# Latent attention: second group's keys scaled ahead of the first group's last two heads, rotated key parts stored with zeros for the neighbouring head

## The chip, the cores and the metric

The kernel runs on one core of one Trainium2 chip. The metric is the device time of one execution in microseconds (us). The kernel before takes 2076.73 us (median of 3 runs, 2075.65 to 2081.17).

## The reference

Two transformer blocks over one sequence of 256 tokens, width 1024, in float32: a short convolution, a dense feed-forward layer, latent attention, a mixture of 8 experts, then feed-forward layers around block attention and a state-space mixer. The change touches latent attention alone:

```python
def mla_mixer(h, cos, sin, w_down, q_a_norm, kv_a_norm, w_uq, w_ukv, q_norm, k_norm, w_o):
    ...
    q = (c_q @ w_uq).reshape(bsz, seq, N_HEADS, QK_HEAD_DIM)          # 8 heads, 128 + 64
    kv = (c_kv @ w_ukv).reshape(bsz, seq, N_HEADS, QK_NOPE_DIM + V_HEAD_DIM)
    k = jnp.concatenate([k_nope, k_rope_h], axis=-1)                  # 64 rotated values, shared
    q = rmsnorm(q, q_norm)
    k = rmsnorm(k, k_norm)
    ...
        scores = jnp.einsum('bqhd,bkhd->bhqk', q[:, s0:end], k[:, :end])
        p = jax.nn.softmax(jnp.where(mask, scores, neg), axis=-1)
        outs.append(jnp.einsum('bhqk,bkhd->bqhd', p, v[:, :end]))
    return o @ w_o
```

A head's score is a product over 128 plain values plus a product over 64 rotated values.

## The kernel before

Projections run as three float32r products of split operands (a high and a low part: ScalarE makes the high part of a weight with a CAST, VectorE the low part with a subtraction, both 128x1024). Scores, transposes and the products with the values run in float32. Every instruction goes through one recording layer, so all of them carry line L149 and are told apart by their tiles.

**Who sets the order.** The order on each engine is fixed when the program is built, by a planner. `Clock` keeps a planned time for each engine; for each recorded instruction it adds a cost from `Clock.cost` (lines 89 to 107) and notes when its tiles are written. For GpSimd (POOL) that cost is the line

```python
        return 0.16 if op == "tensor_scalar" else 0.3 + n * 0.165
```

with n the elements of one partition. `Pipe` (line 276) holds items, each a few stages with names that have to be done first. While the projections are written out, `Pipe.tick` places a stage among them once the planned time says that its inputs are ready (`self.ready(item) <= t["tensor"] + SLACK`). Where a name is needed and nothing is ready, `Pipe.force` places the open stage whose inputs are planned to be ready first. At most 6 items may be started at once. On the chip each engine then runs its instructions strictly in that order; only semaphores make it wait.

**Latent attention** (`mla`, line 1214) takes the heads in two groups g = 0, 1 of four, and the tokens in two tiles t = 0, 1 of 128. For each group: `uq` and `ukv` multiply by the weights, ScalarE evacuates the banks, VectorE sums squares; `norm` then adds two items for each tile. `q_scales` takes roots on POOL and rotates the queries on VectorE; `q_turn` transposes them on TensorE (four 128x128 transposes of the plain parts, two of the rotated parts, two heads in each) and ScalarE copies them to `qn` and `r`. `scales` takes the keys' roots on POOL, `keys` multiplies the keys by them on VectorE, and `turn` transposes the keys to `kn` and `r`.

Each head (`head`, line 1136) has four stages: `scores` (products on TensorE, maximum and bias on VectorE, exponential on ScalarE), `normalise` (VectorE), `transpose` (TensorE, then a copy by VectorE) and `values` (TensorE, then a CAST by ScalarE and a subtraction by VectorE). A score takes for both tiles a product over 128 partitions (`qn`, `kn`), a product over 64 partitions of `r` (partitions 0 to 63 for even heads, 64 to 127 for odd ones), and two bf16 products that add the mask. Line 1439 asks for head 0, and `out_proj` (line 659) multiplies head after head by `w_o` (tile `dn<-s`, 128x512, 12 products for each of heads 0 to 3), waiting for each head by name. The pool of `acc` banks and the pool of `dn` banks have 4 banks each; during `out_proj` the heads use `acc`.

Of the kernel before, what the change touches and what calls it, by code (L numbers as in the profile page):

```python
# [539 lines left out]
class K:  # L540
# [673 lines left out]
    def mla(self, cur, ph):  # L1214
        nc, ws, pipe = self.nc, self.ws, self.pipe
        ws.limit(NSLOT - 7)
        self.lent.clear()
        tsl = lambda t: slice(t * 128, (t + 1) * 128)
# [4 lines left out]
        kr = self.sm([128, 2, 64], "kr")  # L1223
# [47 lines left out]
        for j, n in ((0, 384), (1, 320)):  # L1271
            held = []
            for t in range(2):
                if j == 0 and t:
                    cur.need(1)
                ps = self.lend(("cp", t, j))[:, :n]
                for q in range(4):
                    if t == 0:
                        held.append(ws.get())
                    p = held[q]  # L1280
# [5 lines left out]
        ws.use = 2  # L1286


        q, kv = {}, {}
        rqs = self.sm([128, 2, 8], "rq")  # L1290
        rks = self.sm([128, 2, 8], "rk")
        big = {}

        def tiles(g):
            for t in range(2):
                s = self.slot([128, 1792])
                q[t, g] = s[:, 0:768].rearrange("p (a b) -> p a b", a=4)
                kv[t, g] = s[:, 768:1792].rearrange("p (a b) -> p a b", a=4)

        def uq(g, j):  # L1300
            h = 4 * g + 2 * j
            ps = [self.lend(("uq", t, h))[:, :384] for t in range(2)]
            c = 0
            while c < 3:
                p = ws.get()
                for t in range(2):
                    if g == 0 and j == 0:
                        pipe.need(("lat", t, 0))
                    for i in range(p.n):
                        self.mm3(ps[t], (ch[0][:, c + i, tsl(t)], cl[0][:, c + i, tsl(t)]),  # L1310
                                 (p.h[:, i, :], p.l[:, i, :]), c + i == 0, c + i == 2)
                    pipe.tick()
                c += p.n

            def evac(t):
                qq = q[t, g][:, 2 * j:2 * j + 2, :]

                def copy():
                    nc.scalar.activation(qq, ps[t].rearrange("p (a b) -> p a b", a=2), AF.Copy, scale=ra[:, t, 0:1])

                def squares():
                    for i in range(2):
                        junk = self.t2()
                        nc.vector.scalar_tensor_tensor(junk[:, :192], qq[:, i, :], 1.0, qq[:, i, :], op0=ALU.mult,
                                                       op1=ALU.mult, accum_out=rqs[:, t, h + i:h + i + 1])

                pipe.add([copy], ("uq", t, h), after=(("sq", t, 0),))
                pipe.add([Stage(squares, inputs=lambda: [qq])], ("uqs", t, h), after=(("uq", t, h),))

            for t in range(2):  # L1330
                evac(t)
# [29 lines left out]
        def norm(t, g):  # L1361
            hs = slice(4 * g, 4 * g + 4)
            st = {}

            def q_scales():
                b = rqs[:, t, hs]
                self.rsqrt(b, b, 1.0 / 192)
                nc.gpsimd.tensor_scalar(b, b, 192 ** -0.5, None, op0=ALU.mult)
                st["qr"] = self.t2((128, 4, 64))
                self.rope(st["qr"], q[t, g][:, :, 128:192], tab[:, t, 0], 4, 32)  # L1370

            def scales():
                a = rks[:, t, hs]
                nc.gpsimd.tensor_scalar(a, a, krs[:, t:t + 1], None, op0=ALU.add)
                self.rsqrt(a, a, 1.0 / 192)

            def keys():
                rb = rks[:, t, hs, None]
                kn = kv[t, g][:, :, 0:128]
                nc.vector.tensor_tensor(kn, kn, rb.to_broadcast([128, 4, 128]), op=ALU.mult)  # L1380
                st["kr"] = krh = self.t2((128, 4, 64))
                nc.vector.tensor_tensor(krh, kr[:, t, None, :].to_broadcast([128, 4, 64]),
                                        rb.to_broadcast([128, 4, 64]), op=ALU.mult)

            def rot(n, m):
                src = [st[n][:, 2 * i:2 * i + 2, :] for i in range(2)]
                ps = self.side()
                for i in range(2):
                    nc.tensor.transpose(ps[:, i * 128:(i + 1) * 128], src[i], self.ident)
                nc.scalar.copy(big["r"][:, m, 2 * g:2 * g + 2, tsl(t)],  # L1390
                               ps[:, 0:256].rearrange("p (a b) -> p a b", a=2))

            def q_turn():
                if not big:
                    big["qn"], big["kn"] = self.slot([128, 8, 256]), self.slot([128, 8, 256])
                    big["r"] = self.slot([128, 2, 4, 256])
                self.trans_heads(big["qn"][:, hs, tsl(t)], [q[t, g][:, i, 0:128] for i in range(4)],
                                 lambda o, s: nc.scalar.activation(o, s, AF.Copy, scale=self.gqk))
                rot("qr", 0)

            def turn():
                self.trans_heads(big["kn"][:, hs, tsl(t)], [kv[t, g][:, i, 0:128] for i in range(4)],
                                 lambda o, s: nc.scalar.copy(o, s))
                rot("kr", 1)

            h = 4 * g
            pipe.add([q_scales, q_turn], ("nq", t, g), after=(("uqs", t, h), ("uqs", t, h + 2)))
            pipe.add([scales, keys, turn], ("nk", t, g), after=(("ukvs", t, h), ("ukvs", t, h + 2), ("nq", t, g)))

        out = {}  # L1410

        def score(h, t):
            b = 64 * (h % 2)
            ke = 128 * (t + 1)
            r = big["r"]
            return [(big["qn"][:, h, tsl(t)], big["kn"][:, h, :ke]),
                    (r[b:b + 64, 0, h // 2, tsl(t)], r[b:b + 64, 1, h // 2, :ke])]

        def heads(g):
            if not out:  # L1420
                out["h"], out["l"] = self.slot([128, 8, 256], F32R), self.slot([128, 8, 256], F32R)
            for h in range(4 * g, 4 * g + 4):
                pipe.add(self.head(h, score, [rqs[:, 0, :], rqs[:, 1, :]],
                                   lambda h, kt: kv[kt, h // 4][:, h % 4, 128:256], out["h"], out["l"],
                                   lambda h=h: [big["qn"][:, h, :], big["kn"][:, h, :], big["r"][:, :, h // 2, :]]),
                         (ph, h), after=[(n, t, g) for n in ("nq", "nk") for t in range(2)])

        for g in range(2):
            ws.limit((12, 9)[g], 2)
            tiles(g)  # L1430
            uq(g, 0)
            uq(g, 1)
            ukv(g)
            for t in range(2):
                norm(t, g)
            heads(g)
# [755 lines left out]
```

## Time and profile before

| what | before |
|---|---|
| median of 3 runs | 2076.73 us (2075.65 to 2081.17) |
| profiled execution, its own time | 2080.76 us |
| its span | 2078.9 us |
| TensorE (PE) busy | 2057.5 us (99%) |
| VectorE (DVE) busy | 1480.5 us (71%) |
| ScalarE (ACT) busy | 1164.8 us (56%) |
| GpSimd (POOL) busy | 70.7 us (3%) |
| mean granted TensorE clock | 0.997 of full speed |

PE is busy nearly all the time, so the span is PE's work plus PE's waits. A piece of work off PE counts only where PE waits for it. Latent attention's projections and heads lie between about 292 and 383 us of the span.

### The profile page before, as it was taken

Reading aid. Unit: us, or ns where it says so; the run is one execution under the profiler, and the core shown is the slowest. Engines: PE = TensorE matmul, PEld = TensorE weight load, DVE = VectorE, ACT = ScalarE, POOL = GpSimd, SP = SyncE. Lnnn points to the kernel's source line nnn. Section 1 sums busy time; section 2 is a strip of 40 time slices with the busy share of each in tenths; the row PEclk is TensorE's granted clock in tenths of the full one; section 3 lists DMA queues with packets and bytes.
Section 4 is the critical chain, followed back from the end, with each engine's and each line's share of the span. In section 5 each row is a group of like instructions: output and inputs, shape, how many; then the busy total and the mean of one; then the engine's idle time right before and its main releaser. Section 6 shows DMA issues by size and latency. Waiting matters only on the chain.

```text
span 2078.9 us, 27430 instructions
## 1 busy us (share of the span) xinstructions
PE 2057.5 (99%) x10790; PEld 1752.3 (84%) x10790; DVE 1480.5 (71%) x2051; ACT 1164.8 (56%) x1580; POOL 70.7 (3%) x134
## 2 busy tenths in 40 slices
PE   9999999999999999999999999999999999999999
PEld 9988897888888888887888888888888799988888
DVE  7764567799999999898644787455545588884544
ACT  5444446677777777776544555444444446663442
POOL 0000013000000000000000110000000000010000
PEclk9999999999999999999999999999999999999999
DMA  9565422699999999997856337554655144367530
GB/s 365 189 229 184 147 94 75 241 359 324 372 372 321 374 346 350 375 334 258 306 171 196 126 103 273 188 186 134 231 184 174 50 142 128 117 226 260 183 101 21
DMA packets 203867, 457.81 MB, mean 220 GB/s; under 512 B 10675, under 2 KB 25298, under 8 KB 203730
## 3 DMA queue, kind: packets, MB, share of 16 engines
q1 hardware_dynamic: 203698, 455.97, 62.9%
q8 instruction: 86, 1.41, 0.3%
q14 instruction: 51, 0.42, 0.1%
q10 hardware_dynamic: 32, 0.01, 0.0%
HBM read 454.90 MB, written 1.05 MB: 219 GB/s over the span
## 4 chain that ended last, share of the span: by engine, by line
PE 52%; DVE 0%; ACT 0%; issue 0%; POOL 0%; ACTq 0%
PE acc L149 35%; PE dn L149 17%; ACT s L149 0%; DVE t L149 0%; DVE s L149 0%; POOL gr L149 0%; ACT t L149 0%; DVE x L149 0%; DVE gr L149 0%; DVE pf L149 0%; ACTq L149 0%
## 5 line engine op out<-in xcount | busy, mean ns | idle before, releaser
L149 PE MATMUL acc<-s 128*128 128x512 f32 (+3 forms) x6640 | 1318.7, 356 | 8.5 <-ACT s L149 6.3
L149 PEld LDWEIGHTS acc<-s 128*128 128x128 f32 (+1 forms) x6640 | 1097.1, 189 | 181.5 <-ACT s L149 8.8
L149 DVE TENSOR_TENSOR s<-s 128x1024 fp32r<-128x1024 f32 (+3 forms) x914 | 1041.1, 1184 | 186.2 <-ACT s L149 181.7
L149 ACT CAST s<-s 128x1024 fp32r<-128x1024 f32 (+1 forms) x881 | 867.2, 1040 | 298.1 <-DVE s L149 124.9
L149 PE MATMUL dn<-s 128*128 128x512 f32 (+3 forms) x2888 | 646.6, 381 | 0.2 <-DVE s L149 0.2
L149 PEld LDWEIGHTS dn<-s 128*128 128x128 f32 (+2 forms) x2888 | 507.1, 185 | 102.5 <-issue 3.5
L149 DVE TENSOR_TENSOR s<-acc,s 128x512 fp32r<-128x512 f32 (+1 forms) x102 | 62.2, 635 | 221.3 <-ACT s L149 221.3
L149 ACT ACTIVATE t<-acc,rs 128x512 f32<-128x512 f32 (+1 forms) x68 | 44.3, 657 | 180.9 <-PE acc L149 175.8
L149 DVE SCALAR_TENSOR_TENSOR t<-acc,rs,t 128x512 f32<-128x512 f32 (+1 forms) x60 | 42.2, 705 | 62.9 <-PE acc L149 62.9
L149 ACT CAST s<-acc 128x512 fp32r<-128x512 f32 (+1 forms) x102 | 52.2, 545 | 59.6 <-PE acc L149 59.6
L149 ACT ACTIVATE t<-acc,rsl 128x512 f32<-128x512 f32 x32 | 22.0, 689 | 78.6 <-PE acc L149 78.6
L149 POOL TENSOR_TENSOR rs<-ss 128x1 f32<-128x1 f32 x20 | 5.6, 280 | 1547.1 <-ACT t L149 970.7
L149 PE MATMUL acc<-cst,t 128*128 128x128 f32 x376 | 52.0, 272 | 0.0
L149 PEld LDWEIGHTS acc<-cst,t 128*128 128x128 f32 x376 | 44.7, 140 | 7.4
L149 ACT CAST s<-t 128x512 fp32r<-128x512 f32 (+2 forms) x44 | 26.3, 604 | 41.4 <-DVE t L149 41.2
L149 DVE SCALAR_TENSOR_TENSOR t<-acc,gall,t 128x255 f32<-128x255 f32 (+3 forms) x112 | 42.8, 450 | 6.5 <-ACT t L149 6.4
L149 ACT COPY s<-dn 128x256 f32<-128x256 f32 (+2 forms) x45 | 17.5, 420 | 47.8 <-PE dn L149 47.8
L149 ACT ACTIVATE t<-x 128x512 bf16<-128x512 f32 x40 | 25.1, 628 | 28.3 <-DVE x L149 24.6
L149 DVE TENSOR_TENSOR s<-t,s 128x512 fp32r<-128x512 f32 (+2 forms) x44 | 29.0, 669 | 14.6 <-ACT s L149 14.1
L149 DVE TENSOR_TENSOR t<-acc,gall 128x512 f32<-128x512 f32 x32 | 21.6, 688 | 16.2 <-PE acc L149 16.2
L149 ACT ACTIVATE s<-dn,gall 128x256 fp32r<-128x256 f32 x32 | 13.1, 476 | 26.9 <-PE dn L149 26.9
L149 ACT ACTIVATE t<-t 128x512 f32<-128x512 f32 (+1 forms) x17 | 10.5, 621 | 29.0 <-DVE t L149 29.0
(194 smaller groups left out, 746.9 us busy)
## 6 DMA issues: line engine op xcount, KB each, us to landing
s<-in_moe_w_gate_dram SPq DMA_DIRECT2D x64, 1024.0 KB, 6.1
s<-in_moe_w_up_dram SPq DMA_DIRECT2D x64, 1024.0 KB, 6.2
s<-in_moe_w_down_dram SPq DMA_DIRECT2D x64, 1024.0 KB, 5.3
s<-in_ffn_w_gate_dram SPq DMA_DIRECT2D x55, 1024.0 KB, 5.2
s<-in_ffn_w_up_dram SPq DMA_DIRECT2D x55, 1024.0 KB, 5.2
s<-in_ffn_w_down_dram SPq DMA_DIRECT2D x55, 1024.0 KB, 5.0
s<-in_ssm_w_in_dram SPq DMA_DIRECT2D x24, 1024.0 KB, 5.1
s<-in_attn_w_qkv_dram SPq DMA_DIRECT2D x12, 1024.0 KB, 5.2
```

The costliest lines, as they stand in the source:

```text
L149: return real(out, *args, **kw)
```

## The change

Four edits, all in `mla`:

- Each head's rotated keys get a 128-partition block of their own in `r` (now 8 blocks instead of 4 shared ones): 64 partitions hold the key, the other 64 hold zeros. Two POOL memsets of 64 partitions by 4x256 elements write the zeros once; `turn` writes the keys with two copies of 64 partitions in place of one of 128.
- The rotated queries of two heads stay together in one 128-partition tile, `qr`, which lies in the tile of q and kv (now 2048 elements wide instead of 1792).
- A score's second product so runs over 128 partitions, as the first does; the zeros take out the neighbouring head.
- The keys' item is split: `scales` and `keys` no longer wait for the queries' `q_turn`, and heads 2 and 3 now also wait for `keys` of group 1.

```diff
-                s = self.slot([128, 1792])
+                s = self.slot([128, 2048])
...
+                qr[t, g] = s[:, 1792:2048].rearrange("p (a b) -> p a b", a=2)
...
             def q_turn():
                 if not big:
                     big["qn"], big["kn"] = self.slot([128, 8, 256]), self.slot([128, 8, 256])
-                    big["r"] = self.slot([128, 2, 4, 256])
+
+                    big["r"] = self.slot([128, 8, 256])
+                    pairs = big["r"].rearrange("p (a b) c -> p a b c", b=2)
+                    for i in range(2):
+                        nc.gpsimd.memset(pairs[64 - 64 * i:128 - 64 * i, :, i, :], 0.0)
...
-                rot("qr", 0)
+                nc.scalar.copy(qr[t, g], rot("qr"))
...
-                rot("kr", 1)
+                ps = rot("kr")
+                pairs = big["r"][:, hs, tsl(t)].rearrange("p (a b) c -> p a b c", b=2)
+                for i in range(2):
+                    r = slice(64 * i, 64 * i + 64)
+                    nc.scalar.copy(pairs[r, :, i, :], ps[r])
...
-            pipe.add([scales, keys, turn], ("nk", t, g), after=(("ukvs", t, h), ("ukvs", t, h + 2), ("nq", t, g)))
+            pipe.add([scales, keys], ("keys", t, g), after=(("ukvs", t, h), ("ukvs", t, h + 2)))
+            pipe.add([turn], ("nk", t, g), after=(("keys", t, g), ("nq", t, g)))
...
-                    (r[b:b + 64, 0, h // 2, tsl(t)], r[b:b + 64, 1, h // 2, :ke])]
+                    (qr[t, h // 4][:, h % 4 // 2, :], big["r"][:, h, :ke])]
...
-                         (ph, h), after=[(n, t, g) for n in ("nq", "nk") for t in range(2)])
+                         (ph, h), after=[(n, t, g) for n in ("nq", "nk") for t in range(2)] +
+                         [("keys", t, 1) for t in range(2) if h in (2, 3)])
```

Outside latent attention no engine's order changes, and the order of loads on SP's queue is the same throughout. Three places show what moves.

**PE at head 0's scores.** Before, from the last mask product of head 0 (`dn_3129`) on:

```order
L149 MATMUL dn_3129<-mbf_1321,idbf_1323 128x128
L149 MATMUL dn_3146<-s_2946,s_2945 128x128
L149 MATMUL dn_3146<-s_2946,s_2945 128x256
L149 MATMUL dn_3146<-s_2947 128x128
L149 MATMUL dn_3146<-s_2947 128x256
```

With the change, from the last mask product of head 0 (`dn_3119`) on; `t2_3129` is head 0's exponential, `t2_3143` its transposed copy, `s_2872` its output and `s_3012` the first part of `w_o`:

```order
L149 MATMUL dn_3119<-mbf_1321,idbf_1323 128x128
L149 MATMUL dn_3139<-cst_73,t2_3129 128x128 x3
L149 MATMUL dn_3145<-t2_3143,s_2720 128x256
L149 MATMUL dn_3145<-t2_3143,s_2721 128x128
L149 MATMUL dn_3150<-s_3012,s_2872 128x512 x2
L149 MATMUL dn_3150<-s_3012,s_2873 128x512
```

Before, heads 1, 2 and 3 follow head 0's scores; now head 0's own transposes, values and output products do.

**DVE after the last sum of squares of group 0's keys.** Before (`s<-s,rk` and `t<-kr,rk` are one tile's `keys`, `s<-s 128x1024` the low part of a weight, `SCALAR_TENSOR_TENSOR ..,rq` a head's sum of squares):

```order
L149 TENSOR_TENSOR s<-s,rk 128x4x128
L149 TENSOR_TENSOR t_2962<-kr,rk 128x256
L149 SCALAR_TENSOR_TENSOR t_2964,rq<-s 128x192
L149 SCALAR_TENSOR_TENSOR t_2966,rq<-s 128x192
L149 SCALAR_TENSOR_TENSOR t_2968,rq<-s 128x192
L149 SCALAR_TENSOR_TENSOR t_2970,rq<-s 128x192
L149 TENSOR_TENSOR s<-s 128x1024 x3
L149 TENSOR_TENSOR s<-s,rk 128x4x128
L149 TENSOR_TENSOR t_3034<-kr,rk 128x256
```

With the change:

```order
L149 TENSOR_TENSOR s<-s,rk 128x4x128
L149 TENSOR_TENSOR t_2967<-kr,rk 128x256
L149 TENSOR_TENSOR s<-s,rk 128x4x128
L149 TENSOR_TENSOR t_2991<-kr,rk 128x256
L149 SCALAR_TENSOR_TENSOR t_3004,rq<-s 128x192
L149 SCALAR_TENSOR_TENSOR t_3006,rq<-s 128x192
L149 SCALAR_TENSOR_TENSOR t_3008,rq<-s 128x192
L149 SCALAR_TENSOR_TENSOR t_3010,rq<-s 128x192
L149 TENSOR_TENSOR s<-s 128x1024 x3
L149 SCALAR_TENSOR_TENSOR t_3054,rq<-s 128x192
L149 SCALAR_TENSOR_TENSOR t_3056,rq<-s 128x192
L149 TENSOR_TENSOR s<-s 128x1024 x2
```

Both tiles' `keys` of group 0 now stand together, and five low parts of weights stand ahead of head 0's maximum instead of three.

**DVE behind the last head's scores.** Before (`su` and the tensor-scalar rows normalise a head, `COPY t<-acc` copies a head's transposes, `s<-acc,s` is the low part of a head's output):

```order
L149 RECIPROCAL su<-su 128x2
L149 TENSOR_SCALAR t_3333<-t_3333,su 128x128
L149 TENSOR_SCALAR t_3333<-t_3333,su 128x256
L149 TENSOR_TENSOR s<-s 128x1024
L149 TENSOR_TENSOR s<-acc,s 128x256
L149 COPY t_3410<-acc 128x384
L149 COPY t_3416<-acc 128x384
L149 COPY t_3422<-acc 128x384
L149 TENSOR_TENSOR s<-s 128x1024
L149 TENSOR_TENSOR s<-acc,s 128x256 x3
```

With the change:

```order
L149 RECIPROCAL su<-su 128x2
L149 TENSOR_SCALAR t_3362<-t_3362,su 128x128
L149 TENSOR_SCALAR t_3362<-t_3362,su 128x256
L149 COPY t_3391<-acc 128x384
L149 COPY t_3397<-acc 128x384
L149 COPY t_3403<-acc 128x384
L149 COPY t_3409<-acc 128x384
L149 COPY t_3415<-acc 128x384
L149 COPY t_3421<-acc 128x384
L149 TENSOR_TENSOR s<-acc,s 128x256 x6
```

Six heads (2 to 7) now go through each stage together: on PE six score groups stand in a row, then six groups of transposes, then values of head 2, output products, and the values of heads 3 to 7.

## Rows read from the trace of the kernel before

**Rows 1.** Page, part 1: busy time, share of the span, instructions.
```profile
PE 2057.5 (99%) x10790; PEld 1752.3 (84%) x10790; DVE 1480.5 (71%) x2051; ACT 1164.8 (56%) x1580; POOL 70.7 (3%) x134
```

**Rows 2.** Timeline, PE: start us, us, engine, operation, count, [idle before <-releaser].
```profile
326.72 0.60 PE L149 MATMUL dn<-cst,s 128*128 128x128 f32 x4
...
338.38 0.66 PE L149 MATMUL dn<-cst,s 128*128 128x128 f32 x4 [1.03 <-ACT s L149]
...
341.07 1.72 PE L149 MATMUL dn<-s 128*128 128x128 f32 x8
342.72 0.28 PE L149 MATMUL dn<-mbf,idbf 128*128 128x128 bf16 x2
...
348.17 0.63 PE L149 MATMUL dn<-cst,s 128*128 128x128 f32 x4 [1.60 <-DVE s L149]
...
372.96 2.12 PE L149 MATMUL acc<-t,s 128*128 128x256 f32 x12
374.84 7.76 PE L149 MATMUL dn<-s 128*128 128x512 f32 x33
...
1648.31 0.73 PE L149 MATMUL acc<-s 128*128 128x512 f32 x2 [1.36 <-ACT s L149]
```

**Rows 3.** Windows: stretch, us, busy us of PE, PEld, DVE, ACT, POOL, then PEclk.
```profile
349.00:349.50 0.50, 0.41 (x3) 0.43 (x3) 0.46 (x3) 0.50 (x2) 0.00 (x0) 0.64 0.00 0
...
352.50:353.00 0.50, 0.50 (x4) 0.49 (x4) 0.00 (x0) 0.00 (x0) 0.00 (x0) 0.95 0.00 0
...
1650.00:1652.00 2.00, 2.00 (x9) 1.62 (x7) 0.00 (x0) 0.00 (x0) 0.36 (x1) 0.50 0.00 0
```

**Rows 4.** Groups by line and form, POOL, whole span: busy us, mean ns.
```profile
masks.py:197 POOL MEMSET cst<- 128x128 f32 x1 | 0.2, 204 | 0.3 <-POOLq L2179 0.3
```

**Rows 5.** Timeline, DVE, latent attention.
```profile
327.93 0.68 DVE L149 TENSOR_TENSOR s<-s,rk 128x512 f32<-128x512 f32 x1
...
328.87 0.35 DVE L149 SCALAR_TENSOR_TENSOR t<-s 128x192 f32<-128x192 f32 x1
...
329.98 3.49 DVE L149 TENSOR_TENSOR s<-s 128x1024 fp32r<-128x1024 f32 x3
...
335.44 0.82 DVE L149 TENSOR_TENSOR t<-s 128x256 f32<-128x256 f32 x3
336.30 0.43 DVE L149 TENSOR_TENSOR t<-t,t 128x256 f32<-128x256 f32 x1
...
341.27 0.62 DVE L149 TENSOR_REDUCE mx<-dn 128x1 f32<-128x128 f32 x2 [1.63 <-PE dn L149]
...
351.38 0.55 DVE L149 TENSOR_SCALAR t<-t,su 128x128 f32<-128x128 f32 x2
351.84 0.55 DVE L149 COPY t<-dn 128x384 f32<-128x384 f32 x1
...
374.87 0.43 DVE L149 TENSOR_TENSOR s<-acc,s 128x256 fp32r<-128x256 f32 x1 [0.23 <-ACT s L149]
```

**Rows 6.** Timeline, POOL: the last step of the keys' roots, group 0, tile 1.
```profile
329.08 1.03 POOL L149 TENSOR_TENSOR rk<-rk,mhalf 128x4 f32<-128x4 f32 x1
```

**Rows 7.** Timeline, ACT, latent attention.
```profile
328.19 2.97 ACT L149 CAST s<-s 128x1024 fp32r<-128x1024 f32 x3
331.04 1.07 ACT L149 ACTIVATE s<-acc,mra 128x384 f32<-128x384 f32 x2
...
342.07 1.28 ACT L149 ACT_TABLE_LOAD   x1 [1.77 <-DVE nb L149]
...
344.26 0.20 ACT L149 ACTIVATION_READ_ACCUMULATOR t<-dn,nb,rq 128x1 f32 x1
...
374.46 0.37 ACT L149 CAST s<-acc 128x256 fp32r<-128x256 f32 x1 [0.28 <-PE acc L149]
```

**Rows 8.** Timeline, PEld (weight loads of PE), within head 0's scores.
```profile
340.09 0.52 PEld L149 LDWEIGHTS dn<-s 64*128 64x128 f32 x4 [0.33 <-issue]
340.94 0.11 PEld L149 LDWEIGHTS <-idbf 128*128 128x128 bf16 x2 [0.33 <-issue]
```

More of the change, by code (lines that the diff above doesn't have):

```diff
@@ L1286, in mla @@
         ws.use = 2
-        q, kv = {}, {}
+        q, kv, qr = {}, {}, {}
         rqs = self.sm([128, 2, 8], "rq")
@@ L1383, in keys, with rot @@
                                         rb.to_broadcast([128, 4, 64]), op=ALU.mult)
-            def rot(n, m):
-                src = [st[n][:, 2 * i:2 * i + 2, :] for i in range(2)]
+            def rot(n):
                 ps = self.side()
                 for i in range(2):
-                    nc.tensor.transpose(ps[:, i * 128:(i + 1) * 128], src[i], self.ident)
-                nc.scalar.copy(big["r"][:, m, 2 * g:2 * g + 2, tsl(t)],
-                               ps[:, 0:256].rearrange("p (a b) -> p a b", a=2))
+                    nc.tensor.transpose(ps[:, i * 128:(i + 1) * 128], st[n][:, 2 * i:2 * i + 2, :], self.ident)
+                return ps[:, 0:256].rearrange("p (a b) -> p a b", a=2)
             def q_turn():
@@ L1403, in turn @@
                                  lambda o, s: nc.scalar.copy(o, s))
-                rot("kr", 1)
+                ps = rot("kr")
[3 more added lines that the diff above has]
+                    nc.scalar.copy(pairs[r, :, i, :], ps[r])
             h = 4 * g
             pipe.add([q_scales, q_turn], ("nq", t, g), after=(("uqs", t, h), ("uqs", t, h + 2)))
-            pipe.add([scales, keys, turn], ("nk", t, g), after=(("ukvs", t, h), ("ukvs", t, h + 2), ("nq", t, g)))
+            pipe.add([scales, keys], ("keys", t, g), after=(("ukvs", t, h), ("ukvs", t, h + 2)))
+            pipe.add([turn], ("nk", t, g), after=(("keys", t, g), ("nq", t, g)))
         out = {}
         def score(h, t):
-            b = 64 * (h % 2)
             ke = 128 * (t + 1)
-            r = big["r"]
             return [(big["qn"][:, h, tsl(t)], big["kn"][:, h, :ke]),
-                    (r[b:b + 64, 0, h // 2, tsl(t)], r[b:b + 64, 1, h // 2, :ke])]
+                    (qr[t, h // 4][:, h % 4 // 2, :], big["r"][:, h, :ke])]
         def heads(g):
@@ L1424, in heads @@
                                    lambda h, kt: kv[kt, h // 4][:, h % 4, 128:256], out["h"], out["l"],
-                                   lambda h=h: [big["qn"][:, h, :], big["kn"][:, h, :], big["r"][:, :, h // 2, :]]),
-                         (ph, h), after=[(n, t, g) for n in ("nq", "nk") for t in range(2)])
+                                   lambda h=h: [big["qn"][:, h, :], big["kn"][:, h, :], big["r"][:, h, :], qr[0, h // 4],
+                                            qr[1, h // 4]]),
+                         (ph, h), after=[(n, t, g) for n in ("nq", "nk") for t in range(2)] +
+                         [("keys", t, 1) for t in range(2) if h in (2, 3)])
         for g in range(2):
```

## The prediction

> **What bounds the kernel now.** The page's busy times come first: PE is busy for 2057.5 us, 99% of the span [rows 1]. So I look at PE's work, PE's waits and PE's clock in the stage that the change touches, and at other engines only where PE waits for them. PE's timeline there [rows 2] shows two waits of over 1 us: 1.03 us before group 1's first keys are evacuated (338.38) and 1.60 us before group 1's scaled keys (348.17). The reader is also to see in it a head's scores (341.07 to about 342.85, 1.78 us), three heads' products with the values (372.96 to 374.84, 0.63 us a head) and 33 output products in 7.76 us (0.235 us each). The windows [rows 3] show what followed the 1.60 us wait: the granted clock falls to its lower level (1.2 of 2.4 GHz) for seven half-microseconds, of which the first and the last stand there with 0.64 and 0.95. With 0.50 in the five or so between, about 1.7 us are lost. The same follows the 1.36 us wait at 1648.31: 0.50 in the window from 1650 [rows 2, 3].
>
> **Why the order comes out as it does.** The edit's words promise keys that are ready earlier. But the order is the planner's, and the planner charges a memset by its rule for POOL, 0.3 + 0.165 for each element: 1024 elements make 169 of its microseconds, the two 338. A memset of 128 elements takes 0.204 us on the chip [rows 4]. I estimate 0.2 to 1.6 us each for 1024 elements (as long as that one, or eight times it) and take 1 us; nothing waits for them, since head 0's scores, the first to read the zeros, come some 8 us later. In the planner's books, though, POOL is late by hundreds of microseconds, and so is all that needs group 1's roots. With nothing planned to be ready, stages are placed by force, one head after the other. The order shows it: behind head 0's scores PE gets no other head, but head 0's own transposes.
>
> **The change part by part.** PE's matmuls are the same in number. So the sum is: PE's waits after less waits before, the clock, and what the scores gain. I follow PE from 326.72, up to where both orders agree.
>
> *Turns of group 0.* The four turns now stand together, ahead of the projections that filled the gaps. Six transposes take about 0.7 us (four show 0.60, and ends overlap) [rows 2]. The first queries' turn ends at 327.4; the keys of tile 0 are scaled at 327.93 + 0.68 = 328.6 [rows 5]: 1.1 us wait. Tile 1's keys need POOL's roots, which end at 329.08 + 1.03 = 330.1 [rows 6], and 0.68 us on DVE: 330.8, where PE is ready at 330.0: 0.8 us. Together 1.9 us; PE goes on at 331.5. The four extra 64-partition copies on ACT cost at most the 0.3 us or so of a 128-partition copy each, and are in the next step.
>
> *Banks.* ACT is through with the turns at about 332.3, then makes three casts (2.97 us) before it evacuates group 1's second query bank (1.07 us for two) [rows 7]: 335.8. PE, after six products of 384 columns and twelve of 512, wants that bank at 335.3: 0.5 us. Twelve more products and head 0's scores end at 340.2.
>
> *Head 0, the largest term.* DVE now has to do, from 331.1 on and ahead of head 0's maximum: eight sums of squares of queries (328.87 to 329.98 is four, 1.1 us), five low parts (three take 3.49 us, so 5.8), two rotations (0.82 and 0.43 overlapping, 1.2 us each) and eight shorter sums of squares (at most 0.28 us each, I take 2.0 in all) [rows 5]. That is 12.4 us, and 1 us more until ACT's first cast is there: 344.5. From the start of a maximum to the end of the exponential it is 341.27 to 344.46, 3.2 us with the table load of 1.28 us [rows 5, 7], then 0.6 us until the first half is normalised: 348.3. PE has waited 8.1 us. The copy of the transposes (0.55 us) and the cast of the output (0.37 us) [rows 5, 7] are waited for in turn, with semaphores 1.0 us. Term: 9.1 us. Before, three more heads' scores covered this chain. If DVE were on time, 4.9 us would be left.
>
> *Head 1.* Its chain without the table load takes 1.9 + 0.6 us; two queries' turns of group 1 (1.4 us) lie beside it. Left are 1.1 us, then copy and cast, 1.0 us, and 0.2 us for the second tile's keys, which DVE scales only then: 2.3 us.
>
> *Heads 2 to 7.* Six score groups stand in a row and PE is busy. Call their end T. DVE then takes the last maximum and bias (0.9 us) and normalises six heads at 0.65 us each (0.46 us between the rows at 351.38 and 351.84, and a reciprocal) [rows 5]. PE waits 1.5 us for the first, 0.3 us for each of the next three. The fifth head's transposes need a bank that DVE's copy of the first frees, and DVE makes that copy only after the sixth normalisation, at T + 5.4: 1.5 us. Then 0.2 us for banks, 0.45 us for a cast, and 0.25 us for the low part of head 2's output, which stands behind all six copies (T + 8.15). Term: 4.8 us.
>
> *Clock.* The fall behind the 1.60 us wait goes with it. The waits at head 0 and behind T are longer than the two that a fall followed [rows 2, 3]; I take two falls, 1.7 us each: 3.4 in place of 1.7. Bounds: none to four, 0 to 6.8 us.
>
> *Scores.* The 64-partition group begins after a gap of 0.33 us in the weight loads, and the mask's loads come after another [rows 8]. Without the change of shape a head could take two times the 0.63 us that the products with the values take for the same 128 + 256 columns, and 0.13 us for the mask: 1.39 for 1.78 us [rows 2]. Bounds 0 and 0.39 us a head; I take 0.39, since that row is of the same size and operand type, for the seven heads on PE's path (head 0's is hidden behind DVE): 2.7 us.
>
> A rule speaks against the padding. The Trainium skill, TensorEngine Tiling (Array Packing), Overview, gives up to twice the speed to products over 64 rows or fewer. By that rule the zeros would give away half of the 0.85 us that a 64-row group takes, 3.4 us over 8 heads, where I count a gain of 2.7. The trace doesn't bear it out: the group takes 0.85 us (340.09 to 340.94), more than 0.63 [rows 2, 8].
>
> **The sum.** Waits after: 1.9 + 0.5 + 9.1 + 2.3 + 4.8 = 18.6 us. Waits before: 1.03 + 1.60 = 2.6. So +16.0; the clock +1.7; the scores -2.7: **+15.0 us**. The profiled execution took 2080.76 us, 4.0 more than the median of 2076.73, and would come to 2095.8. Set on the median: **2091.7 us**. Later stages keep their order, and PE is their bound, so nothing is won back.
>
> **The rivals.**
> - *Faster.* The short scores (8 x 0.39 = 3.1 us) and the end of the two waits and of the clock's fall (1.03 + 1.60 + 1.7) decide: 2076.7 - 7.4 = 2069.3 us. It needs DVE to be through with its list when head 0's scores end, and a softmax chain below 1 us. The rows make it 3.8 us, and nothing stands beside it on PE. Chance 0.04.
> - *No difference to be measured* (0.3%, 6.2 us, is about what a measurement can tell). DVE is on time (head 0: 4.9), head 1 costs 1, the tail 2, no clock fall: 10.3 - 2.6 - 1.7 - 2.7 = +3.3, 2080.0 us. Against it stands DVE's list. Chance 0.09.
> - *The clock stays low.* With wait after wait, the lower level lasts from head 0 into head 1, and 7 us of work there take 14: 2099 us. For it: both the 1.36 and the 1.60 us wait were followed by a fall, and the new ones are longer. Chance 0.11.
> - *Narrow products are fast.* The rule on 64 rows holds: 15.0 + 2.7 + 3.4 = +21.1, 2097.8 us. Against it stands the row. Chance 0.03.
> - *The memsets are as slow as planned.* Head 0's scores wait: some 2410 us. Against it stand the 0.204 us. Chance 0.01.
>
> **How the numbers follow.** The forecast keeps 0.72. Its own bounds are the head 0 term without DVE's lag and no fall (+7, 2084) and four falls with no gain in the scores (+21, 2098). The range of 2083 to 2102 takes in the low clock and the narrow products, and leaves out 0.14. Faster by over 0.3%: 0.04; within: 0.09; slower: 0.87.
>
> **What would show it.** Right: a PE wait of some 8 us for DVE (`t`) just behind head 0's scores, with no other head between; DVE busy meanwhile with low parts and squares; a row of waits behind the last scores; 64-row loads gone and heads 1.4 us apart; memsets of about 1 us. Wrong: DVE's maximum right behind head 0's scores, waits below 10 us in all between 326 and 395, or a span that grows outside that stretch.

## The result, and the profile after

The changed kernel took 2098.32 us (median, 2096.24 to 2099.43), the kernel before beside it 2078.53 us: a ratio of 1.0094, 95% interval [1.0082, 1.0106], or 19.8 us more. The forecast was 15.0 us more. The profiled execution took 2097.98 us with a span of 2096.2, 17.3 us over the span before.

The page's busy times say little. PE has 5 us more, ACT's extra instructions are the half-width copies, POOL has the two memsets:

```profile
PE 2062.4 (98%) x10790; PEld 1757.8 (84%) x10790; DVE 1480.9 (71%) x2051; ACT 1166.9 (56%) x1584; POOL 72.7 (3%) x136
```

PE's timeline of the stage, where [rows 2] stood before (start us, us, engine, operation, count, idle before and what ended it):

```profile
325.86 0.60 PE L149 MATMUL dn<-cst,s 128*128 128x128 f32 x4
...
327.81 0.66 PE L149 MATMUL dn<-cst,s 128*128 128x128 f32 x4 [1.13 <-DVE s L149]
...
330.44 0.63 PE L149 MATMUL dn<-cst,s 128*128 128x128 f32 x4 [1.10 <-DVE s L149]
...
335.95 3.03 PE L149 MATMUL acc<-s 128*128 128x512 f32 x12 [0.84 <-ACT s L149]
338.82 1.47 PE L149 MATMUL dn<-s 128*128 128x128 f32 x8
340.13 0.27 PE L149 MATMUL dn<-mbf,idbf 128*128 128x128 bf16 x2
348.18 0.95 PE L149 MATMUL dn<-cst,t 128*128 128x128 f32 x3 [7.77 <-DVE t L149]
349.78 1.65 PE L149 MATMUL dn<-t,s 128*128 128x256 f32 x4 [0.65 <-DVE t L149]
351.89 4.21 PE L149 MATMUL dn<-s 128*128 128x512 f32 x12 [0.46 <-ACT s L149]
...
359.49 0.44 PE L149 MATMUL acc<-cst,t 128*128 128x128 f32 x2 [0.87 <-ACT t L149]
...
374.24 1.53 PE L149 MATMUL acc<-s 128*128 128x128 f32 x8
...
375.72 1.53 PE L149 MATMUL acc<-s 128*128 128x128 f32 x8
...
380.23 2.20 PE L149 MATMUL acc<-cst,t 128*128 128x128 f32 x9 [1.40 <-DVE t L149]
...
392.65 7.54 PE L149 MATMUL dn<-s 128*128 128x512 f32 x32
```

The reader is to see the long wait of 7.77 us straight behind head 0's scores, the two at the turns (1.13, 1.10), the 1.40 us behind six heads' scores in a row, and heads that follow each other after 1.48 us (374.24 to 375.72), where a head took 1.78 [rows 2].

What DVE did meanwhile, and the memsets on POOL (timelines of DVE and POOL, same columns; low parts from 333.43 and 337.40, a rotation at 340.23, the maximum only at 344.39):

```profile
333.43 3.50 DVE L149 TENSOR_TENSOR s<-s 128x1024 fp32r<-128x1024 f32 x3 [1.69 <-ACT s L149]
...
337.40 2.35 DVE L149 TENSOR_TENSOR s<-s 128x1024 fp32r<-128x1024 f32 x2
...
340.23 0.82 DVE L149 TENSOR_TENSOR t<-s 128x256 f32<-128x256 f32 x3
...
344.39 0.61 DVE L149 TENSOR_REDUCE mx<-dn 128x1 f32<-128x128 f32 x2
```

```profile
329.62 1.95 POOL L149 MEMSET s<- 64x1024 f32 x2
```

The granted clock in windows of 5 us (columns as in [rows 3]):

```profile
345.00:350.00 5.00, 1.17 (x4) 0.69 (x5) 1.47 (x7) 2.38 (x5) 2.47 (x4) 0.50 0.63 231
350.00:355.00 5.00, 4.54 (x12) 3.46 (x13) 1.65 (x2) 1.31 (x2) 0.00 (x0) 0.56 0.00 0
355.00:360.00 5.00, 4.06 (x27) 3.20 (x25) 1.31 (x7) 1.66 (x6) 0.00 (x0) 1.00 0.01 2
360.00:365.00 5.00, 3.69 (x11) 2.69 (x12) 2.26 (x6) 2.44 (x6) 0.00 (x0) 0.63 0.00 0
365.00:370.00 5.00, 5.00 (x24) 4.34 (x23) 1.95 (x3) 2.43 (x6) 0.00 (x0) 0.69 0.00 0
...
380.00:385.00 5.00, 3.78 (x16) 2.44 (x17) 4.82 (x21) 2.08 (x8) 0.00 (x0) 0.68 0.00 0
385.00:390.00 5.00, 4.54 (x18) 3.64 (x16) 1.85 (x5) 1.31 (x2) 0.00 (x0) 0.64 0.00 0
```

Three falls to the lower level, where the forecast had two. PE's busy time in each window times what is missing of the clock to 1.00 gives 2.6, 2.9 and 2.8 us: 8.3 us lost, an estimate from the windows' means. The mean granted clock of all four executions of the change, 0.992 to 0.994, is below that of the kernel before, 0.997 in its profile. (In the kernel before the same windows show 3.31 us busy at 0.91 and 5.00 at 0.74: 1.6 us.)

From the first turn to the point where both kernels turn x for the next part, PE took 75.8 us (325.86 to 401.62) where it had taken 55.7 (326.72 to 382.44): 20.0 us more, so all of the loss lies in this stage. The rest of the span is 2.8 us shorter in this execution than in the one profiled before: 0.9 us ahead of the stage and 1.9 behind it, where the clock was low for less time (by the same estimate, in windows of 10 us, 2.8 us lost for 4.3).

### The profile page after: what moved, and what is told of

The parts are those of the page before. It is cut to its first block, busy times and chain, and to the rows that moved or that the text cites. A ratio compares the mean times of both kernels' runs of the same rounds, so it can differ in the third digit from the quotient of the medians.

```text
span 2096.2 us, 27450 instructions
## 1 busy us (share of the span) xinstructions
PE 2062.4 (98%) x10790; PEld 1757.8 (84%) x10790; DVE 1480.9 (71%) x2051; ACT 1166.9 (56%) x1584; POOL 72.7 (3%) x136
## 4 chain that ended last, share of the span: by engine, by line
PE 52%; DVE 0%; ACT 0%; POOL 0%; issue 0%; ACTq 0%
PE acc L149 35%; PE dn L149 17%; ACT s L149 0%; DVE t L149 0%; DVE s L149 0%; POOL gr L149 0%; ACT t L149 0%; DVE x L149 0%; DVE gr L149 0%; DVE pf L149 0%; ACTq L149 0%
## 5 line engine op out<-in xcount | busy, mean ns | idle before, releaser
L149 PE MATMUL dn<-s 128*128 128x512 f32 (+3 forms) x2832 | 636.9, 383 | 1.6 <-ACT s L149 1.4
L149 PEld LDWEIGHTS dn<-s 128*128 128x128 f32 (+1 forms) x2832 | 501.4, 185 | 102.2 <-ACT s L149 2.3
L149 PE MATMUL acc<-cst,t 128*128 128x128 f32 x393 | 57.3, 278 | 3.4 <-DVE t L149 2.1
L149 ACT COPY s<-dn 128x256 f32<-128x256 f32 (+3 forms) x41 | 15.5, 405 | 47.3 <-PE dn L149 47.3
```

Source lines behind the costliest of these rows:

```text
L149: return real(out, *args, **kw)
```

## The experiments

The forecast named one cause, the planner's price of a memset. The rival was that other parts of the change do the harm whatever the price. So the parts were taken singly and together. Ratios are to the kernel before, timed beside each run; a price is in the planner's microseconds.

| kernel | keys split from their turn | heads 2, 3 wait for group 1's keys | price of a memset | ratio | 95% interval |
|---|---|---|---|---|---|
| the change | both groups | yes | 169 us | 1.0094 | 1.0082 to 1.0106 |
| e1 | both | yes | 1 us | 1.0059 | 1.0045 to 1.0072 |
| e5 | both | no | 169 us | 1.0070 | 1.0056 to 1.0083 |
| e6 | both | no | 1 us | 1.0033 | 1.0021 to 1.0045 |
| e12 | group 0 | no | 1 us | 1.0031 | 1.0021 to 1.0041 |
| e9 | group 1 | yes | 1 us | 1.0015 | 1.0005 to 1.0024 |
| e10 | group 1 | head 3 alone | 1 us | 1.0020 | 1.0011 to 1.0029 |
| e3 | none | no | 169 us | 1.0023 | 1.0013 to 1.0032 |
| e2 | none | no | 1 us | 0.9992 | 0.9983 to 1.0001 |
| e4 (no zeros, no memset) | both | yes | none | 1.0080 | 1.0066 to 1.0094 |

**The price alone (e1).** In the changed kernel, L107:

```diff
-        return 0.16 if op == "tensor_scalar" else 0.3 + n * 0.165
+        return 0.16 if op == "tensor_scalar" else 1.0 if op == "memset" else 0.3 + n * 0.165
```

> The changed kernel with one number of the planner corrected: a POOL memset is charged 1 us (what the two took each) in place of 0.3 + 0.165 for each element. The same instructions, in another order. Theory A (the wrong price sets an order that leaves PE waiting): PE gets projections and head 1's scores between head 0's scores and its transposes, the 7.8 us wait for t and the three falls of the clock go, and the time is the kernel before's less 2 to 8 us (2069 to 2075 against 2077), ratio 0.996 to 0.999. Theory B (zeros, four half-width copies or the split itself cost the time): at most 3 us better than the change, ratio to the kernel before 1.006 or more.

Measured: 1.0059, between the two and next to theory B's bound. The order did change as theory A has it: projections and head 1's scores now stand behind head 0's. But only 0.0035, 7 us of 19.5, came back, and of the three falls of the clock one stays (0.77 and 0.55 in the windows from 345 and 350). The timeline of PE shows what is left:

```profile
327.99 0.66 PE L149 MATMUL dn<-cst,s 128*128 128x128 f32 x4 [1.14 <-DVE s L149]
...
330.62 0.63 PE L149 MATMUL dn<-cst,s 128*128 128x128 f32 x4 [1.10 <-DVE s L149]
...
345.46 0.44 PE L149 MATMUL dn<-cst,t 128*128 128x128 f32 x2 [2.94 <-DVE t L149]
...
376.26 1.01 PE L149 MATMUL acc<-cst,t 128*128 128x128 f32 x6 [2.77 <-DVE t L149]
```

The waits at the turns stand there unchanged, and the wait behind six heads in a row has grown to 2.77 us. Neither comes from the price.

**The padding alone (e2), and with the old price (e3).** Keys, turn and heads as in the kernel before:

```diff
-            pipe.add([scales, keys], ("keys", t, g), after=(("ukvs", t, h), ("ukvs", t, h + 2)))
-            pipe.add([turn], ("nk", t, g), after=(("keys", t, g), ("nq", t, g)))
+            pipe.add([scales, keys, turn], ("nk", t, g), after=(("ukvs", t, h), ("ukvs", t, h + 2), ("nq", t, g)))
...
-                         (ph, h), after=[(n, t, g) for n in ("nq", "nk") for t in range(2)] +
-                         [("keys", t, 1) for t in range(2) if h in (2, 3)])
+                         (ph, h), after=[(n, t, g) for n in ("nq", "nk") for t in range(2)])
```

> The padding alone with the corrected price: keys are not split from their turn, and no head waits for group 1's keys; PE's order is that of the kernel before, row for row. Theory A: only the scores change. Eight heads gain 0.30 us each (1.78 to 1.475): 2.4 us faster, ratio 0.9988, between 0.998 and 1.000. Theory B (padding costs, through ACT's half-width copies or wider products): 2 us slower or more, ratio above 1.001. Rival by the rule on narrow products: 3.4 us slower, 1.0016.

> As the padding alone, but with the planner's own price of 169 us for each memset. The turns of group 0 move behind the projections, but four heads' scores still stand in a row ahead of head 0's transposes. Theory A (the price does its harm mostly together with the split, which lets heads 0 and 1 run ahead alone): no wait of 7.8 us, 0 to 8 us slower than the kernel before, ratio 1.000 to 1.004. Rival A2 (the price alone is enough): 12 to 22 us slower, ratio 1.006 to 1.0106.

Measured: 0.9992 for e2, 1.7 us faster, as theory A has it, with an interval that just reaches no change. The slower time of 1.0016 that the rival expected lies outside the interval: the zeros give away nothing. The rival applied the rule on narrow products (the Trainium skill, TensorEngine Tiling (Array Packing), Overview) to single products; the page promises the speed to independent tiles of the array, so the run refutes that use of the rule and not the page. In the kernel before, all 64-row products of one head lie on the same 64 partitions. e3 lies at 1.0023, inside the bounds of theory A, but not for its reason. There is a long wait, at the turn of group 0's first keys, which DVE now scales behind the rotations, at 341.96, and the whole chain behind it waits less:

```profile
342.70 1.12 PE L149 MATMUL dn<-cst,s 128*128 128x128 f32 x4 [7.28 <-DVE s L149]
```

e2 against e3 is the price by itself: 0.0031, 6.4 us, much the same as with the split (7.3 from e1, 7.7 from e6 to e5). The sentence in e3's expectation that the price needs the split falls.

**The split alone (e4).** Into the kernel before, without zeros and without memset:

```diff
-            pipe.add([scales, keys, turn], ("nk", t, g), after=(("ukvs", t, h), ("ukvs", t, h + 2), ("nq", t, g)))
+            pipe.add([scales, keys], ("keys", t, g), after=(("ukvs", t, h), ("ukvs", t, h + 2)))
+            pipe.add([turn], ("nk", t, g), after=(("keys", t, g), ("nq", t, g)))
...
-                         (ph, h), after=[(n, t, g) for n in ("nq", "nk") for t in range(2)])
+                         (ph, h), after=[(n, t, g) for n in ("nq", "nk") for t in range(2)] +
+                         [("keys", t, 1) for t in range(2) if h in (2, 3)])
```

> The split of the keys from their turn alone, with the wait of heads 2 and 3 for group 1's keys; the rotated parts as in the kernel before, no memset. Theory A: the 1.60 us wait and the clock's fall behind it go (3.3 us), new short waits take up to 3: between 4 us faster and 2 us slower, ratio 0.998 to 1.001. Theory B (the split leaves PE waiting whatever the price is): 10 us slower or more, ratio above 1.005.

Measured: 1.0080, and theory A missed it by far. With no memset in the program, most of the loss is there. Theory B holds for the split together with its wait. The waits of PE in this stage, by what ended them (us in total, how often, the longest) add up to 13 us, and none is the 7.8 us one:

```profile
PE acc L149 <- DVE t L149: 2.8, 1, 2.8
PE acc L149 <- ACT s L149: 2.3, 1, 2.3
PE dn L149 <- DVE s L149: 2.2, 2, 1.1
PE dn L149 <- DVE t L149: 2.2, 2, 2.0
PE dn L149 <- DVE su L149: 1.5, 1, 1.5
PE acc L149 <- DVE s L149: 1.2, 1, 1.2
PE dn L149 <- ACT s L149: 0.9, 2, 0.5
```

**Without the wait of heads 2 and 3 (e5, e6).** In the changed kernel, in e6 with the price of e1 too:

```diff
-                         (ph, h), after=[(n, t, g) for n in ("nq", "nk") for t in range(2)] +
-                         [("keys", t, 1) for t in range(2) if h in (2, 3)])
+                         (ph, h), after=[(n, t, g) for n in ("nq", "nk") for t in range(2)])
```

> The change without the new wait of heads 2 and 3 for group 1's keys; the planner's price of a memset as in the change. Theory W (that wait does most of the harm, since it keeps heads 2 and 3 behind both tiles' keys and so leaves heads 0 and 1 uncovered and puts six heads in one row) together with theory A (the price places head 0 alone): head 0's wait of 8 us stays, the waits behind six heads in a row shrink to 1 or 2 us; 6 to 14 us slower than the kernel before, ratio 1.003 to 1.007. Rival S (the split of the turns itself costs the time): ratio 1.008 or more.

> The change without the new wait of heads 2 and 3 and with the memset charged 1 us: four heads' scores stand in a row ahead of head 0's transposes again, the turns of group 0 still stand together. Theories W and A: the waits at the turns (1.1, 1.1 and 0.9 us) stay, head 0's goes, the scores gain 2.4: between 3 us faster and 4 us slower than the kernel before, ratio 0.9985 to 1.002. Rival S (the turns together and what follows cost the time): 8 us slower or more, ratio 1.004 or more.

Measured: 1.0070, the upper bound of theories W and A, and 1.0033, between what they and rival S gave, so neither suffices. The wait is worth 0.0024 and 0.0026, some 5 us, with either price. What e6 keeps over e2, 0.0041 or 8.5 us, is the split's own. Its timeline shows where: after four heads' scores in a row, PE waits for group 1's queries, whose rotations DVE now does at 347.49, behind the maxima. In e2 they stand at 335.49, ahead of them (PE of e6, DVE of e6, DVE of e2):

```profile
348.91 0.41 PE L149 MATMUL dn<-cst,t 128*128 128x128 f32 x2 [3.31 <-ACT s L149]
```

```profile
345.19 0.62 DVE L149 TENSOR_REDUCE mx<-dn 128x1 f32<-128x128 f32 x2 [0.66 <-PE dn L149]
...
347.49 0.82 DVE L149 TENSOR_TENSOR t<-s 128x256 f32<-128x256 f32 x3
```

```profile
335.49 0.82 DVE L149 TENSOR_TENSOR t<-s 128x256 f32<-128x256 f32 x3
```

The row names ACT's s as the last to come (an evacuation of an `acc` bank on ACT ended at about 348.8). But the tile that PE transposes there is DVE's rotated one, whose last step ended at 348.76, 0.15 us ahead of PE. The three waits ahead of the scores come on top (1.13, 1.10 and 0.87 us, as in the change). In all, PE's waits between 324 and 390 us come to 9.8 us in e6 and 3.5 in e2, and the granted clock falls to 0.66 in the window from 350 in e6 and stays at 1.00 in e2.

**One group's split at a time (e9, e10, e12).** From e1 (e9 with the wait of heads 2 and 3, e10 with head 3's alone, e12 with none and with the two branches the other way round):

```diff
+            if g == 0:
+                pipe.add([scales, keys, turn], ("nk", t, g), after=(("ukvs", t, h), ("ukvs", t, h + 2), ("nq", t, g)))
+            else:
+                pipe.add([scales, keys], ("keys", t, g), after=(("ukvs", t, h), ("ukvs", t, h + 2)))
+                pipe.add([turn], ("nk", t, g), after=(("keys", t, g), ("nq", t, g)))
```

> Only the second group's keys are split from their turn; the first group's stay in one stage as in the kernel before. Heads 2 and 3 wait for the second group's keys, zeros are stored, a memset is charged 1 us. Theory G (the split costs through the first group: its four turns stand together ahead of the projections and wait 1.1, 1.1 and 0.9 us, and its rows on DVE come later): group 0's turns stand as before, waits in the stage come to 3 to 5 us, between 4 us faster and 3 us slower than the kernel before, ratio 0.998 to 1.0015. Rival W (the wait of heads 2 and 3 costs 5 us wherever group 0's turns stand): ratio 1.002 or more.

> As the split of the second group's keys alone, but only head 3 waits for them: three heads' scores ahead of the second group's turns. Theory G: within 2 us of that run, ratio 0.998 to 1.0015; if it beats the padding alone (0.9992), it is the best version. Rival W: 2 to 3 us better than the run in which heads 2 and 3 wait, and still slower than the padding alone.

> Only the first group's keys are split from their turn, memset charged 1 us, zeros stored, no head waits for the second group's keys. Theory G (the split of the first group makes its four turns stand together, with waits of 1.1, 1.1 and 0.9 us, and puts DVE's low parts and sums of squares behind them): nearly all of the 8.5 us by which the run without the wait (1.0033) stands above the padding alone (0.9992) comes back: ratio 1.002 to 1.0045. Rival (it is the second group's split that costs): ratio 0.998 to 1.001.

Measured: 1.0031 for e12, 8.1 of the 8.5 us: it is the first group's split that costs, as theory G has it, and e12 has e6's waits at the turns and at the rotated queries (1.13, 1.10, 0.88 and 3.31 us). e9, 1.0015, is at the upper edge of theory G, with 5.9 us of waits where 3 to 5 were expected. e10, 1.0020, lies above the theory's range, and 1 us above e9 where rival W had it 2 to 3 us below. They stand 5 and 6 us above e2. As e6 and e12 differ by 0.4 us, with some 3 us of uncertainty, the second group's split costs nothing that shows there, so the 5 us are put down to the wait; the second group's split by itself, without any wait, was not run. Nor does the wait remove the 1.60 us wait for the second group's keys. PE's timeline of e10 has it one head earlier, with a new wait behind it:

```profile
346.03 0.63 PE L149 MATMUL dn<-cst,s 128*128 128x128 f32 x4 [1.61 <-DVE s L149]
...
356.49 1.67 PE L149 MATMUL dn<-cst,t 128*128 128x128 f32 x6 [2.02 <-ACT t L149]
```

**Keys early by hand (e11).** From e2; group 1's keys, tile 0, behind the maxima of head 1, tile 1 behind head 2's (their `scales` are an item of their own, for which these heads wait):

```diff
+                early[(1, 2)[t]] = lambda: (keys(), pipe.done.add(("kd", t)))
+                pipe.add([turn], ("nk", t, g), after=(("kd", t), ("nq", t, g)))
...
+                f = st[0].fn
+                st[0].fn = lambda f=f, h=h: (f(), early.pop(h, lambda: 0)())
```

> The padding alone (memset charged 1 us), with group 1's keys scaled on DVE straight behind the maxima of heads 1 and 2 instead of behind head 3's; PE's order up to the second group's turns is that of the kernel before. Theory D (the 1.60 us wait at the turn is DVE's order alone): that wait goes, PE comes to head 0's transposes about 1.6 us earlier and waits about 1 us there for the normalised products, since DVE has the same rows to do: 0 to 2 us faster than the padding alone, ratio 0.998 to 0.9995. Rival: the maxima come later by the keys' 1.1 us and push the normalisation back: as the padding alone or up to 3 us slower, ratio 0.9995 to 1.001.

Measured: 1.0004 [0.9995, 1.0013], in the rival's range. The first half of theory D holds: the 1.60 us wait is gone, and 0.87 us at the softmax stands in its place. But a wait that no theory had takes more than was won: DVE does two low parts (351.48, 2.36 us) before the next two heads' maxima, ACT waits 2.16 us for them, and its cast of head 0's output, which PE's next products need, stands behind both heads' exponentials (PE's timeline, then ACT's):

```profile
348.05 2.27 PE L149 MATMUL dn<-cst,t 128*128 128x128 f32 x11 [0.87 <-ACT t L149]
...
356.94 2.93 PE L149 MATMUL dn<-s 128*128 128x512 f32 x6 [2.70 <-ACT s L149]
```

```profile
354.55 0.46 ACT L149 ACTIVATE t<-dn,nb,rq 128x128 f32<-128x128 f32 x1 [2.16 <-DVE nb L149]
...
356.52 0.37 ACT L149 CAST s<-dn 128x256 fp32r<-128x256 f32 x1
```

No version here beats the kernel before by more than the measurement can tell; the padding alone (e2) is the best.

**The clock (e7, e8).** In the changed kernel, products of ones into head 0's bank, in columns that nothing reads (`mla_out` picks latent attention's heads):

```diff
+            if oh is self.mla_out and h == 0:
+                for i in range(54):
+                    nc.tensor._real.matmul(ps[:, 384:512], self.ones, self.ones, start=True, stop=True)
```

(32 in e8.)

> The change with 54 products of 128 columns of ones put into PE's order in the long wait behind head 0's scores (some 0.125 us each, 6.8 of the 7.8 us), into columns of head 0's bank that nothing reads. Theory C (the falls of the clock cost some 5 us more than forecast, and the first follows the idle stretch): no 0.50 between 345 and 354 us, the next twelve output products take 2.9 in place of 4.21 us, the time is 3 to 5 us below the change's, ratio to the kernel before 1.007 to 1.008 (the change 1.0094). Rival: the clock falls all the same, or the products only put the wait elsewhere: ratio 1.0088 or more.

> The change with 32 products of ones in head 0's wait. The profile of the run with 54 shows two rows for each product and 12.28 us for all, so that they ran 4.5 us past the wait; 32 take 7.3 us and fit into its 7.8. Theory C: the clock stays up behind the wait (no 0.50 from 345 to 355), head 0's wait is no longer than before, and the time is 4 to 7 us below the change's: ratio to the kernel before 1.006 to 1.0075 (the change 1.0094). Rival: the low clock cost next to nothing there, since PE waits on other engines in that stretch anyway: ratio 1.0085 or more.

Measured: 1.0088 [1.0074, 1.0102] and 1.0086 [1.0072, 1.0100], neither told apart from the change by its time. Both profiles tell more (PE's timeline of e7, then of e8):

```profile
340.58 12.28 PE L1180 MATMUL dn<-ones 128*128 128x128 f32 x108
352.69 0.49 PE L149 MATMUL dn<-cst,t 128*128 128x128 f32 x3
...
355.21 3.03 PE L149 MATMUL dn<-s 128*128 128x512 f32 x12 [0.46 <-ACT s L149]
...
391.42 9.11 PE L149 MATMUL dn<-s 128*128 128x512 f32 x39
```

```profile
340.86 7.36 PE L1180 MATMUL dn<-ones 128*128 128x128 f32 x64
348.82 0.70 PE L149 MATMUL dn<-cst,t 128*128 128x128 f32 x3 [0.60 <-DVE t L149]
...
351.56 4.52 PE L149 MATMUL dn<-s 128*128 128x512 f32 x12 [0.46 <-ACT s L149]
```

In e7 the fill ran past the wait and took 12.28 us, not 6.8. Head 0's transposes begin 4.5 us later than in the change, yet from there to the output products PE takes 38.7 us (352.69 to 391.42) where the change takes 44.5 (348.18 to 392.65). The work and its order are the same, and the twelve products take 3.03 for 4.21 us. PE's waits in between are no shorter (6.7 us for 6.0), so the 5.8 us are low clock: in e7 it stays at 1.00 up to 380 us and falls once behind that, to 0.84 and 0.82 in the windows from 380 and 385. The fill's overrun of 4.5 us takes most of it back, which leaves the time at the rival's bound. In e8 the fill fits into the wait and the twelve products take 4.52 us all the same: the clock fell a little later, behind the waits of 0.60, 0.65 and 0.46 us (0.66 in the window from 350, and again in the one from 360; the third fall is gone). So e7's profile bears out what theory C says the clock costs. What it expected of a fill that fits into this one wait did not come, and by their times alone neither rival is excluded.

## Why the prediction was right, and where its reasons were not

**Side, size and place** came out: slower, 19.8 for 15.0 us, all of it between the first turn and the output products.

**The waits** were found one by one. Turns: 2.2 us measured for 1.9. Banks: 0.8 for 0.5. Head 0: 7.77 + 0.65 + 0.46 = 8.9 for 9.1. Head 1: 2.2 for 2.3. Behind six heads in a row: 2.7 us in named waits for 4.8. Together 16.9 for 18.6. DVE's list ahead of head 0's maximum ended at 344.4, where 344.5 was forecast.

**The scores** gained 0.30 us a head for 0.39: the loads of 64 rows are gone, but a head takes 1.475 us and not 1.39. That is 2.4 us over eight heads.

**The clock** is the term that was mis-sized: "I take two falls, 1.7 us each: 3.4 in place of 1.7." There were three, and they cost 8.3 us in place of 1.6. The 1.7 was read from one fall behind a single 1.60 us wait with PE busy after it; here each fall has more short waits behind it and lasts longer (by windows of half a microsecond some 10, 7 and 7 us, against 3.4 in the kernel before). That one fills eight half-microseconds, six of them at 0.50, and not seven and five; the 1.7 is right for six. The rival that the clock stays low came nearest by its number, 2099 us, but not by its picture: the clock was back at 1.00 from 355 to 360 us and fell again twice. The bounds of 0 to 6.8 us were too narrow. The forecast also left out a third wait of the kernel before, 0.34 us for ACT at the banks (331.69). With 8.3, 2.4 and this wait in the sum, the terms give 16.9 - 3.0 + 6.7 - 2.4 = 18.2 us of the 20.0 in this stage. The other 1.8 us were not traced; some lie inside grouped rows, such as the nine transposes of 2.20 us (1.93 in e8 at the full clock, 1.15 in the kernel before).

**The cause** was the step that failed. "In the planner's books, though, POOL is late by hundreds of microseconds [...]. With nothing planned to be ready, stages are placed by force, one head after the other." That is true of head 0's 7.8 us (gone in e1 and e4, there in e5), and it was told as the reason for everything. The runs put the loss together from four parts, each in us of 2077: the split 8.5 (e2 to e6; 8.1 of it in e12, with the first group's alone), the price 7.3 (e1 to the change), the wait of heads 2 and 3 5.4 (e6 to e1), the padding -1.7 (e2). They add up to 19.5, as they must, since each step starts where the last one ended. Three runs off this path test the sum: e3 comes to 4.8 us where the parts give 5.6, e5 to 14.5 for 14.1, e4 to 16.6 for 13.9. Each difference of two ratios is uncertain by about 0.0018, or 4 us, so the three sums hold within it, and the order of the first three parts is not settled; that none of these three is zero is, since each shows in two or three pairs.

The order of the instructions showed the forecast what would wait, so the sum came out. It did not show why the order was so, and correcting the price, which the forecast's text would have had anyone do, gives back hardly more than a third. The clue was there: four turns in a row, ahead of the projections, are early work, not work placed by force. With the split they stand there at either price (e1, e5); with the wrong price and no split the keys' turns stand behind the projections (e3). On the chip the keys still stood behind a low part and POOL's roots, for which DVE waited 1.51 us; what time the planner had down for them, no run shows.

## What to carry to other kernels

When a planner orders the work, its new order tells what will wait, not which edit made it so. Take the edits singly before naming one. Splitting a stage in two gives the planner a new place for every instance of it: here what was meant was the second group's keys, and the first group's split cost 8 us. A wait written into the program to get something early is paid for by what it holds back, here the scores that covered another head's softmax.

## What the chip showed that was not expected

**The lower clock outlasts an idle stretch, and filling a wait doesn't always prevent it.** In the change it was already at 0.50 when PE resumed (348.18) and stayed there for six us more; in e8, with no idle stretch over 0.65 us behind the fill, it fell all the same.

**The same wait is followed by a fall in one execution and not in another.** In e2 and e9 PE's rows up to 341 us are the same, with waits of 1.27 and 0.27 us in e2 and 1.28 and 0.27 in e9. The windows that follow (e2, then e9):

```profile
340.00:345.00 5.00, 5.00 (x34) 4.39 (x35) 1.96 (x10) 3.53 (x9) 2.66 (x5) 1.00 0.05 18
345.00:350.00 5.00, 3.31 (x25) 2.63 (x23) 4.27 (x17) 4.54 (x16) 0.00 (x0) 1.00 0.01 2
```

```profile
340.00:345.00 5.00, 4.66 (x20) 3.74 (x20) 1.12 (x6) 2.10 (x4) 2.56 (x5) 0.68 0.42 158
```

And e2's wait of 1.60 us in the second row, after which the kernel before fell to 0.50 [rows 2, 3], brought none. A clock term behind waits of one or two us is a chance, not a price, and single profiles differ by it.

**A memset of 64x1024 elements on POOL takes 0.98 us**, 4.8 times the 0.204 us of 128x128 [rows 4], for eight times the elements of a partition.
